# Decoder step on one core: the samples' softmax tail in more pieces, the first mixer chunk and a memory weight split among the sample batches, the last sum of squares behind the first query

## The chip, the core and the metric

The kernel runs on one core of a Trainium2 chip. The core has five engines that work side by side and wait for each other by semaphores: TensorE (PE, matrix products and transposes, with its weight loads listed as PEld), VectorE (DVE), ScalarE (ACT), GpSimd (POOL) and SyncE (SP), which here issues nearly all DMAs. Matrix products write into PSUM, a small memory of eight banks that PE, DVE and ACT can reach. Everything else works in SBUF, 128 partitions wide. Each engine takes its instructions in a fixed order, so an instruction that waits holds up all that is behind it on that engine.

The metric is the time of one execution on the device, in microseconds (us). The median of three runs before the change is 1881.3 us (1880.76 to 1881.76).

## The reference

One layer of a hybrid decoder, for a prompt of 1024 tokens and for eight samples of four new tokens each, 1056 tokens together, with a model width of 1024. All is float32. What matters here:

```python
def rms_norm(x, g):
    xf = x.astype(jnp.float32)
    y = xf * lax.rsqrt(jnp.mean(xf * xf, axis=-1, keepdims=True) + EPS)
    return (y * g.astype(jnp.float32)).astype(x.dtype)

def masked_attend(q, k, v, q_pos, k_pos):
    s = jnp.einsum('...qhd,...khd->...hqk', q, k).astype(jnp.float32) * (QK_HEAD ** -0.5)
    s = jnp.where(k_pos[None, :] <= q_pos[:, None], s, NEG_INF)
    p = jax.nn.softmax(s, axis=-1).astype(v.dtype)
    return jnp.einsum('...hqk,...khd->...qhd', p, v)

def mla_sample_attend(q, ckv_n, kpe, pool_ckv, pool_kpe, page_table, w_uk, w_uv, g_qk_k):
    ...
    def one(args):
        pages, q1, c1, pe1 = args
        c_all = jnp.concatenate([pool_ckv[pages].reshape(PAST_LEN, KV_LORA), c1.astype(pool_ckv.dtype)], axis=0)
        pe_all = jnp.concatenate([pool_kpe[pages].reshape(PAST_LEN, QK_ROPE), pe1.astype(pool_kpe.dtype)], axis=0)
        k, v = mla_keys_values(c_all, pe_all, k_pos, w_uk, w_uv, g_qk_k)
        return masked_attend(q1, k, v, q_pos, k_pos)

def merge_out(a_out, b_out, g_out_a, g_out_b, w_o):
    return jnp.concatenate([rms_norm(a_out, g_out_a), rms_norm(b_out, g_out_b)], axis=-1) @ w_o

def mem_kv(mem, g_mem_in, w_mk, w_mv, g_mk):
    n, m, _ = mem.shape
    hm = rms_norm(mem, g_mem_in)
    k = rms_norm((hm @ w_mk).reshape(n, m, MEM_HEADS, MEM_HEAD_DIM), g_mk)
    v = (hm @ w_mv).reshape(n, m, MEM_HEADS, MEM_HEAD_DIM)
    return k, v

def mem_attend(h, mk, mv, w_mq, g_mq, w_mo):
    n, t, _ = h.shape
    q = rms_norm((h @ w_mq).reshape(n, t, MEM_HEADS, MEM_HEAD_DIM), g_mq)
    ...
```

For each sample the keys of 4096 past positions are rebuilt from paged latents (32 pages of 128 positions), normalised per head and compared with the four new queries of eight heads. The layer then merges the gMLP group (a) and the attention group (b) through `w_o`, attends to 256 memory tokens (`mem_kv`, `mem_attend`), and ends in a gated feed-forward with a short convolution.

## The kernel before

**Precision.** A product in full float32 is made of three products of split operands: each operand is a rounded high half and a low half (the remainder), and `mm3` (L185) adds high x high, high x low and low x high. The high half is a copy on ACT (L191, or L195 with a gain), the low half a subtraction on DVE (L192, L198). So each operand must be split before PE can use it.

**Stages in order of time.** The input projections and the gMLP group (`phase1`), the prompt's attention (`phase2a`), the samples' attention in eight batches of 16 steps (`phase2b`), the memory's keys and values (`mem_kv`), the mixed output projection (`mixed`, `out_proj`), the memory attention (`mem_attention`), the feed-forward (`ffn`).

**The sample loop.** A batch is one sample. A page holds 128 positions and is called a group; a step treats two groups, four pages make a quad (two steps). In `phase2b` the order on PE, ACT, DVE and POOL is written out by hand: `at(n, pos, f)` puts a piece of work at step n and at a position within it (from -2 to 3; the scores stand between 1 and 2, the products with the values between 2 and 3). The order on SP is left to a planner. Per step: PE makes the scores from the quad's split latents (tiles ch for the high, cl for the low half, against w2h and w2l) into the PSUM tiles s; ACT squares them (L1272, L1275), DVE adds the rope part (L1274) and reduces the squares (L1278). Per quad: four page loads each of cT (transposed latents, three buffers) and ck (latents as values, a ring of fifteen buffers), the cast to ch on ACT (L1231), the subtraction to cl half on POOL and half on DVE (L1235), and the key rotation krq on POOL (L1220 to L1222). PE reads POOL's half of cl in the third matmul of a quad's first step.

**The softmax of a batch** is `batch_softmax`, in pieces r = 0 to 10 at steps counted from the batch's first. The norms of the first 24 groups come at steps 12 to 14, their scaling on POOL at 14 (L1296), their peak at 15. The last eight groups' norm starts at 16; at position 2 of step 16 it is finished, with scaling, peak and maximum (mx, L1323). PE transposes the peaks at the start of step 18 (L1326), DVE reduces them at its end, and at the end of step 19 PE spreads the maximum to all partitions (L1334), ACT copies it (L1336) and POOL subtracts it from the scores (L1337, 128 x 1056). ACT takes the exponential at step 20. Since a batch has 16 steps, steps 16 to 20 lie in the next batch. The products with the values follow four steps after the batch, from step 23 on (L1346, L1348). The last batch's pieces behind step 16 run after the loop.

**Between the stages.** The mixers' outputs go through a DRAM tensor (`mix_dram`, written by `mix_steps` in pairs of token tiles, L1505). After the loop, `mem_kv` begins: the memory weights' tiles and the memory itself are loaded into four places of the ck ring in the last steps (L1113). `mixed` then loads `mix_dram` back in three chunks of 384, 384 and 288 tokens (L1530, three `raw` buffers shared with the weights) and splits them into mx0, mx1 and mx2. `out_proj` runs over the eight output tiles, for each the three chunks, adds the squares of the result per chunk in `acc` (ACT L1591, POOL L1592), and at its end makes the sums over the width for all three chunks on PE (L270) and their inverse roots `r3` on DVE (`rsqrt`, L222 to L236), in the PSUM banks o, m and o again. `mem_attention` starts with `query(0, 0)`, whose PSUM tile b takes over the bank o.

## Time and profile before

| | us |
|---|---|
| median of three runs | 1881.3 |
| profiled execution, its own time | 1887.48 |
| its span, first to last instruction | 1885.8 |
| TensorE busy | 1822.9 |
| the sample loop, about 427 to 892 | 465 |
| memory keys and values, to the first chunk of the mixer, about 892 to 934 | 42 |
| mixed output projection, to the first query, about 934 to 1042 | 108 |

The profile is of one execution, and its rows use its own clock from the first instruction. In a row of the timeline stand the start, the duration, the engine, the line, the operation, the tile written and the tiles read; in square brackets stand the engine's idle time before it and what ended it. "A <- B" in a list of waits says that A waited for B. TensorE's granted clock was 0.985 of full speed on average over the span. Where the prediction needs lines, they are shown there.

### The profile page before, as it was taken

To read this page: it belongs to the slowest core of one execution; us is meant where nothing else is said; L and a number is where in the kernel's file an instruction comes from. 1 tells how busy PE (TensorE), PEld (TensorE's weight loads), DVE (VectorE), ACT (ScalarE), POOL (GpSimd) and SP (SyncE) were. 2 spreads that over 40 slices of the span, in tenths; PEclk is the share of its full clock that TensorE was granted. 3 is DMA by queue.
4 is the path that set the end of the run, shared out by engine and by line. 5 is a ranking of instruction groups with operands and counts; after the bars stand their busy time and mean duration, and the time that the engine had idled before them with its cause. 6 is when DMAs were issued, how large, how long until landed. Compare 5 with 4: busy or idle time off the path is not lost.

```text
span 1885.8 us, 39848 instructions
## 1 busy us (share of the span) xinstructions
PE 1822.9 (97%) x14402; PEld 1757.2 (93%) x14402; DVE 1380.2 (73%) x2883; ACT 927.5 (49%) x1965; POOL 715.1 (38%) x826
## 2 busy tenths in 40 slices
PE   6999899989999999999999999999999999999999
PEld 6999799889999999998799988999999999999999
DVE  6865967766777667776654676788888888879664
ACT  6435676666555555555443355633332333344442
POOL 1221515643544455444213100157677677500000
PEclk9999899999999999999999999999999999999999
DMA  8102204666765665664564335322222222395252
GB/s 294 60 10 69 80 1 163 228 223 186 213 196 167 187 179 169 175 170 148 171 177 134 134 134 163 128 80 69 91 69 94 77 69 80 99 363 164 79 153 76
DMA packets 135559, 260.18 MB, mean 138 GB/s; under 512 B 20417, under 2 KB 78626, under 8 KB 132290
## 3 DMA queue, kind: packets, MB, share of 16 engines
q1 hardware_dynamic: 134498, 256.58, 43.4%
q8 instruction: 114, 1.87, 0.4%
q10 hardware_dynamic: 864, 1.05, 0.2%
q14 instruction: 83, 0.68, 0.1%
HBM read 212.27 MB, written 45.30 MB: 137 GB/s over the span
## 4 chain that ended last, share of the span: by engine, by line
PE 60%; DVE 6%; issue 4%; DMA 3%; POOL 2%; SPq 1%; ACT 1%; POOLq 0%; DVEq 0%; ACTq 0%
PE d L185 12%; PE s L185 11%; PE b L185 7%; PE F L185 7%; PE X L185 6%; PE E L185 6%; PE A L185 3%; PE y L185 3%; DMA cT<-cT 1%; PE o L1348 1%; DVE mx L1299 1%; POOL S L1296 1%; PE t L185 1%; PE v L185 1%; SPq L1207 1%
## 5 line engine op out<-in xcount | busy, mean ns | idle before, releaser
L185 PE MATMUL s<-w2h,ch 128*128 128x288 f32 (+1 forms) x1024 | 303.8, 297 | 0.0
L185 PE MATMUL s<-w2h,cl 128*128 128x288 f32 (+1 forms) x1024 | 295.1, 288 | 2.7 <-POOL cl L1235 1.4
L185 PE MATMUL s<-w2l,ch 128*128 128x288 f32 (+1 forms) x1024 | 294.7, 288 | 0.0
L185 PEld LDWEIGHTS s<-w2h,ch 128*128 128x128 f32 x1024 | 192.6, 188 | 10.8 <-issue 8.3
L185 PEld LDWEIGHTS s<-w2h,cl 128*128 128x128 f32 x1024 | 192.4, 188 | 3.4 <-POOL cl L1235 1.9
L185 PEld LDWEIGHTS s<-w2l,ch 128*128 128x128 f32 x1024 | 192.8, 188 | 0.0
L1278 DVE TENSOR_REDUCE ss<-sq 128x16 f32<-128x1024 f32 x128 | 155.6, 1215 | 49.3 <-ACT sq L1275 48.4
L1235 POOL TENSOR_TENSOR cl<-cT,ch 128x512 fp32r<-128x512 f32 x64 | 83.7, 1307 | 160.7 <-ACT ch L1231 128.9
L1275 ACT ACTIVATE sq<-s 128x512 f32<-128x512 f32 x128 | 76.5, 598 | 90.0 <-PE s L185 90.0
L1272 ACT ACTIVATE sq<-s 128x512 f32<-128x512 f32 x128 | 76.8, 600 | 78.0 <-PE s L185 78.0
L191 ACT CAST a<-brb 128x528 fp32r<-128x528 f32 x77 | 48.8, 634 | 111.0 <-PE d L185 107.1
L185 PE MATMUL mm<-whi,xh 128*128 128x256 f32 (+3 forms) x288 | 84.5, 294 | 14.4 <-ACT xh L195 9.8
L185 PE MATMUL d<-a,w 128*128 128x264 f32 x768 | 95.4, 284 | 1.0 <-DVE G L2064 1.0
L192 DVE TENSOR_TENSOR a<-brb,a 128x528 fp32r<-128x528 f32 x77 | 54.4, 707 | 57.2 <-ACT a L191 57.1
L185 PEld LDWEIGHTS d<-a,w 128*128 128x128 f32 x768 | 94.3, 188 | 1.1 <-issue 1.1
L185 PE MATMUL mm<-wlo,xh 128*128 128x256 f32 (+3 forms) x288 | 83.3, 292 | 0.0
L185 PE MATMUL mm<-whi,xl 128*128 128x256 f32 (+3 forms) x288 | 83.2, 293 | 0.0
L930 PEld LDWEIGHTS o<-v,pth 128*128 128x128 f32 x576 | 75.9, 197 | 7.3 <-ACT pth L920 5.2
L930 PE MATMUL o<-v,pth 128*128 128x64 f32 x576 | 76.2, 274 | 4.8 <-ACT pth L920 4.4
L1935 POOL TENSOR_TENSOR lo<-s,hi 128x1024 fp32r<-128x1024 f32 x20 | 63.0, 3148 | 45.7 <-ACT hi L1934 45.7
L1231 ACT CAST ch<-cT 128x512 fp32r<-128x512 f32 x128 | 73.5, 627 | 3.9 <-DMA cT<-cT 3.9
L1990 ACT COPY a<-A 128x264 f32<-128x264 f32 x43 | 16.1, 375 | 118.7 <-PE A L185 114.9
(714 smaller groups left out, 6472.2 us busy)
## 6 DMA issues: line engine op xcount, KB each, us to landing
cT<-cT SPq DMA_DIRECT2D x256, 160.0 KB, 2.5
ck<-ck SPq DMA_DIRECT2D x256, 144.0 KB, 3.4
raw<-w_up SPq DMA_DIRECT2D x44, 512.0 KB, 3.6
wsumd<-wsum SPq DMA_DIRECT2D x13, 1024.0 KB, 4.3
actd<-cv SPq DMA_DIRECT2D x44, 264.0 KB, 2.6
brb<-actd SPq DMA_DIRECT2D x44, 264.0 KB, 5.9
wsum<-w_down SPq DMA_DIRECT2D x11, 1024.0 KB, 5.2
raw<-wsumd SPq DMA_DIRECT2D x20, 512.0 KB, 3.8
```

Source lines behind the costliest of these rows:

```text
L185: self.nc.tensor.matmul(out, l, r, start=first and i == 0, stop=last and i == len(seq) - 1)
L191: {"act": nc.scalar.copy, "pool": nc.gpsimd.tensor_copy, "dve": nc.vector.tensor_copy}[eng](hi, src)
L192: low = lambda: nc.vector.tensor_tensor(lo, src, hi, ALU.subtract)
L930: nc.tensor.matmul(u["o"][:, e], th[:, z * P : z * P + P], s["v"][:, jj, h % 4], start=j == z == 0, stop=e == 1 and jj == 2 * G + 1)
L1207: nc.sync.dma_start(ck[j * 32 : j * 32 + 32], I["ck"][bass.ds(rv, 1)].rearrange("a t s f -> (a t) s f"))
L1231: nc.scalar.copy(d["h"][:, k], src[k])
L1235: (nc.vector if k else nc.gpsimd).tensor_tensor(d["l"][:, k], src[k], d["h"][:, k], ALU.subtract)
L1272: nc.scalar.activation(sq[:, 0], ps[:, :, n0 : n0 + 256], AF.Square)
L1275: nc.scalar.activation(sq[:, 1], pt.rearrange("p (e d) -> p e d", e=2), AF.Square)
L1278: yield lambda: nc.vector.tensor_reduce(s["ss"][:, g0 : g0 + 2].rearrange("p e (z h) -> p z e h", z=2), sq.rearrange("p z e (h d) -> p z e ...
L1296: e.tensor_tensor(x, x, ss[:, g0:g1].rearrange("p g h -> p (g h)").unsqueeze(2).broadcast_to([P, n, 4]), ALU.mult)
L1935: eng.tensor_tensor(lo, src, hi, ALU.subtract)
```

## The change

1. `batch_softmax` has thirteen pieces instead of eleven. The last eight groups' norm starts at step 16, has its second part at the start of 17, its third at the end of 17, and scaling, peak and maximum come at the end of step 18. The transpose moves to step 19, the reduction of the peaks to 20, the spreading with POOL's subtraction to the end of step 20, the exponential to step 21. The closing of a batch's output moves by one step.
2. The first mixer chunk (mx0) is loaded and split in the sample loop: four loads into the ck ring at steps 20, 36, 52 and 68, eight splits at relative steps 8 and 10 of the batches that follow. `mixed` leaves it out. The first memory weight is loaded first of the four last loads and split two steps before the loop's end. `mix_steps` writes each token tile to DRAM by itself.
3. The sums and roots of the third chunk leave `out_proj` and stand behind `query(0, 0)`, in another PSUM bank; its `acc` lies in another pool. In `mem_kv` the ring of diagonal tiles has three buffers instead of four, and two small tiles of the samples' memory attention share a buffer with another.

```diff
@@ phase2b
-        hl = self.t(p, [P, 4, 288], F32, "ck", 15).rearrange("p k n -> p (k n)")[:, :1024].rearrange("p (k n) -> p k n", k=4)
+        hl = self.t(p, [P, 4, 288], F32, "ck", 15).rearrange("p k n -> p (k n)")[:, :1024].rearrange("p (m k n) -> p m k n", m=2, k=4)
+        hl = [hl[:, i] for i in range(2)]
...
+        self.mx0 = [self.t(px, [P, 8, 384], FR, f"mx0{x}") for x in "hl"]
+        wk0 = [self.t(px, [P, 8, P], FR, f"wk0{x}") for x in "hl"]
...
+        place = lambda: self.t(p, [P, 4, 288], F32, "ck", 15).rearrange("p k n -> p (k n)")
+
+        def mixed_load(k):
+
+            raw = place()[:, :768].rearrange("p (k n) -> p k n", k=2)
+            nc.sync.dma_start(raw, self.mix_dram[:, k : k + 2, :384])
+            for e in range(2):
+                at(8 * k + 24 + 2 * e, 3, lambda e: self.split(*(x[:, k + e] for x in self.mx0), raw[:, e], self.col("g_ab", k + e)), e)
+
+        for k in range(0, 8, 2):
+            at(8 * k + 20, 0, mixed_load, k)
+        at(last - 2, 3, lambda: self.split(*wk0, raws[0].rearrange("p (k n) -> p k n", k=8)))
...
-            for r, (k, pos) in enumerate(((12, 0), (13, 0), (14, 0), (14, 3), (15, 0), (16, 0), (16, 2), (18, 0), (18, 3), (19, 2), (20, 2))):
+            for r, (k, pos) in enumerate(((12, 0), (13, 0), (14, 0), (14, 3), (15, 0), (16, 0), (17, 0), (17, 3), (18, 2), (19, 2), (20, 0), (20, 2), (21, 3))):
...
-            for k, pos, f in ((0, 3, tail[0]), (1, 2, tail[1]), (3, 3, tail[2])):
+            for k, pos, f in ((0, 3, tail[0]), (2, 2, tail[1]), (4, 3, tail[2])):
...
-                    src = (I["memT"][:, :4], I["memT"][:, 4:], I["w_mk"][0], I["w_mk"][1])[len(raws)]
+                    src = (I["w_mk"][0], I["memT"][:, :4], I["memT"][:, 4:], I["w_mk"][1])[len(raws)]
@@ batch_softmax
         elif r == 5:
             s["it"] = norms(24, 32, nc.gpsimd if final else nc.vector)
             next(s["it"])
+        elif r == 6:
             next(s["it"])
-        elif r == 6:
+        elif r == 7:
             for _ in s["it"]:
                 pass
+        elif r == 8:
             scale(nc.vector, 24, 32)
             peak(1, 24, 33)
...
@@ mem_kv
-            w = self.stream(I["w_mk"][h], 8, raw=raws[2 + h].rearrange("p (k n) -> p k n", k=8) if h < 2 else None)
+            w = wk0 if h == 0 else self.stream(I["w_mk"][h], 8, raw=raws[3].rearrange("p (k n) -> p k n", k=8) if h == 1 else None)
...
-                dg = self.t(p, [P, P], F32, "diag", 4)
+                dg = self.t(p, [P, P], F32, "diag", 3)
@@ mix_steps
-            nc.vector.tensor_copy(hl[:, :, i * tn : i * tn + tn], tp)
+            nc.vector.tensor_copy(hl[i][:, :, :tn], tp)
+            o = t0 + i * tn
+            nc.sync.dma_start(self.mix_dram[:, z * 4 : z * 4 + 4, o : o + tn], hl[i][:, :, :tn])
             if nt is None and i < m - 1:
                 yield
-        nc.sync.dma_start(self.mix_dram[:, z * 4 : z * 4 + 4, t0 : t0 + w], hl[:, :, :w])
@@ mixed
-                for k in range(0, 8, 2):
+                for k in range(0, 8 if c else 0, 2):
@@ out_proj
-        for c in range(3):
-            st = self.t(self.ppt, [P, 512], F32, "om"[c % 2], 1)
-            self.tok_sums(st, acc[c], c, self.ones)
-            ct = slice(3 * c, 3 * c + 3)
-            self.rsqrt(p, r3[:, ct], st[:, ct], 1.0 / 1024)
+        for c in range(2):
+            self.token_roots(p, self.t(self.ppt, [P, 512], F32, "om"[c], 1), r3, c)
+
+    def token_roots(self, p, st, r3, c):
+        self.tok_sums(st, self.acc[c], c, self.ones)
+        ct = slice(3 * c, 3 * c + 3)
+        self.rsqrt(p, r3[:, ct], st[:, ct], 1.0 / 1024)
@@ mem_attention
+        roots = self.t(pp, [P, 512], F32, "sx", 1)
...
                 if h == 0 and c == 0:
+                    self.token_roots(p, roots, r3, 2)
                     memory()
```

More of the change, by code (lines that the diff above doesn't have):

```diff
@@ L487, in mix @@
         def mix(i0):
-            hl = self.t(pl, [P, 4, 256], F32, "hl")
+            hl = self.t(pl, [P, 2, 4, P], F32, "hl")
+            hl = [hl[:, i] for i in range(2)]
             self.mix_group(pl, pp, 0, i0, min(i0 + 2, 9), lambda i: a_all[:, i], hl, lambda j: self.t(pl, [P, 512], F32, "csq", 4), ("st", 3))
@@ L701, in mix @@
                 hl = hls.pop()
+                hl = [hl[:, :, a : a + P] for a in (0, P)]
                 nt = lambda j: self.t(p, [P, 2, 4, 96], F32, "k", 4).rearrange("p m h d -> p (m h d)")[:, :512]
@@ L1050, in phase2b @@
         pa = self.pa3 = self.open("p3a", side="right")
-        pt, p = self.open("p3t"), self.open("p3")
+        pt, px, p = self.open("p3t"), self.open("mx"), self.open("p3")
+        self.mx0 = [self.t(px, [P, 8, 384], FR, f"mx0{x}") for x in "hl"]
+        wk0 = [self.t(px, [P, 8, P], FR, f"wk0{x}") for x in "hl"]
         ppt, pp = self.open("ps3t", space=PSUM), self.open("ps3", space=PSUM)
@@ L1071, in run @@
                 f()
-        hl = self.t(p, [P, 4, 288], F32, "ck", 15).rearrange("p k n -> p (k n)")[:, :1024].rearrange("p (k n) -> p k n", k=4)
+        hl = self.t(p, [P, 4, 288], F32, "ck", 15).rearrange("p k n -> p (k n)")[:, :1024].rearrange("p (m k n) -> p m k n", m=2, k=4)
+        hl = [hl[:, i] for i in range(2)]
         mix = self.mix_steps(pa, ppt, 1, 6, 8, lambda i: self.b_last[:, i % 2], hl, None, ("m", 1))
@@ L1110, in steps @@
                 if n > last - 8 and n % 2 == 0 and len(raws) < 4:
-                    raw = self.t(p, [P, 4, 288], F32, "ck", 15).rearrange("p k n -> p (k n)")[:, : 8 * P]
-                    src = (I["memT"][:, :4], I["memT"][:, 4:], I["w_mk"][0], I["w_mk"][1])[len(raws)]
+                    raw = place()[:, : 8 * P]
+                    src = (I["w_mk"][0], I["memT"][:, :4], I["memT"][:, 4:], I["w_mk"][1])[len(raws)]
                     nc.sync.dma_start(raw.rearrange("p (k n) -> p k n", n=src.shape[2]), src)
@@ L1145, in phase2b @@
             self.wp = self.open("w", bufs=3, side="right")
-            mem = self.mem_kv(raws)
+            mem = self.mem_kv(raws, wk0)
             for f in late:
@@ L1323, in batch_softmax @@
             nc.vector.tensor_tensor(s["m"][:, 0], s["m"][:, 0], s["m"][:, 1], ALU.max)
-        elif r == 7:
+        elif r == 9:
             tp = s["tp"] = self.t(pp, [P, 512], F32, "m", 1)
             nc.tensor.transpose(tp[:32, :P], s["m"][:, 0], self.ident)
-        elif r == 8:
+        elif r == 10:
             mm = self.t(p, [32, 1], F32, "mm", 2)
@@ L1331, in batch_softmax @@
             nc.vector.tensor_scalar(s["dg"], self.ident[:32, :32], mm, None, ALU.mult)
-        elif r == 9:
+        elif r == 11:
             bc = self.t(pp, [P, 512], F32, "m", 1)[:, :32]
@@ L1385, in stream, with mem_kv @@
         return hi, lo
-    def mem_kv(self, raws):
+    def mem_kv(self, raws, wk0):
         nc, tc, I, O = self.nc, self.tc, self.I, self.O
@@ L1397, in mem_kv @@
         acc = self.t(p, [P, 256], F32, "acc")
-        mr = [r.rearrange("p (k n) -> p k n", k=4) for r in raws[:2]]
+        mr = [r.rearrange("p (k n) -> p k n", k=4) for r in raws[1:3]]
         xs = [(mh[:, k], ml[:, k]) for k in range(8)]
@@ L1488, in mix_steps @@
             ns.append(n)
-            o = n if nt else hl[:, 2 * (i - i0) : 2 * (i - i0) + 2].rearrange("p k n -> p (k n)")[:tn]
+            o = n if nt else hl[i - i0][:tn].rearrange("p k n -> p (k n)")
             nc.scalar.activation(o, src(i)[:tn], AF.Square, accum_out=r[:, i - i0 : i - i0 + 1])
@@ L1492, in mix_steps @@
         self.rsqrt(p, r, r, 1.0 / 512)
-        w = m * tn
         yield
@@ L1501, in mix_steps @@
                 nc.tensor.transpose(tp[:, k], n[:, k * P : k * P + P], self.ident[:tn, :tn])
-            nc.vector.tensor_copy(hl[:, :, i * tn : i * tn + tn], tp)
+            nc.vector.tensor_copy(hl[i][:, :, :tn], tp)
+            o = t0 + i * tn
+            nc.sync.dma_start(self.mix_dram[:, z * 4 : z * 4 + 4, o : o + tn], hl[i][:, :, :tn])
             if nt is None and i < m - 1:
                 yield
-        nc.sync.dma_start(self.mix_dram[:, z * 4 : z * 4 + 4, t0 : t0 + w], hl[:, :, :w])
     def mixed(self):
         nc, I = self.nc, self.I
-        px = self.open("mx")
         pm = self.pm = self.open("pm")
-        mxs = [None] * 3
-        for c in (0, 2, 1):
+        mxs = [self.mx0, None, None]
+        for c in (2, 1):
             o, n = CH[c]
             if c == 1:
-                self.acc = [self.t(pm, [P, 384], F32, f"acc{e}") for e in range(3)]
+                self.acc = [self.t(pm, [P, 384], F32, f"acc{e}") for e in range(2)]
                 self.t(pm, [P, 384], F32, "sqx", 3)
-            mxs[c] = [self.t(px if c == 0 else pm, [P, 8, n], FR, f"mx{c}{x}") for x in "hl"]
+            mxs[c] = [self.t(pm, [P, 8, n], FR, f"mx{c}{x}") for x in "hl"]
         ws = {}
@@ L1708, in sample_values @@
                 nc.tensor.transpose(tp[:, k], sample["p"][:, 0, k * P : k * P + P], self.ident)
-            pT = self.t(ps_, [P, 2, P], F32, "pT")
+            pT = self.t(ps_, [P, 1, 256], F32, "pf").rearrange("p a (k n) -> p (a k) n", k=2)
             nc.vector.tensor_copy(pT, tp)
@@ L1725, in sample_values @@
                         )
-            sd = self.t(ps_, [P, P], F32, "sd")
+            sd = self.t(ps_, [P, 1, 256], F32, "pf")[:, 0, :P]
             nc.scalar.copy(sd, so)
@@ L2238, in build @@
     r3 = N.t(xp, [P, 9], F32, "r3")
+    N.acc.append(N.t(xp, [P, 384], F32, "acc2"))
     po = N.open("po")
```

## The prediction

> **What bounds the kernel now.** The first view is the page: span and the engines' busy row.

> ```profile
> span 1885.8 us, 39848 instructions
> PE 1822.9 (97%) x14402; PEld 1757.2 (93%) x14402; DVE 1380.2 (73%) x2883; ACT 927.5 (49%) x1965; POOL 715.1 (38%) x826
> ```

> TensorE (PE) is busy for 1822.9 of 1885.8 us. The change adds and removes no matmul, so it can act in only two ways: on the 62.9 us in which PE stands idle, and on the stretches in which PE is busy at a lower granted clock. The second view is therefore the list of PE's waits (who waited for whom: total, times, longest).

> ```profile
> PE m L1326 <- DVE mx L1323: 6.3, 7, 0.9
> PE b L185 <- DVE r L236: 2.7, 1, 2.7
> PE b L185 <- DVE ml L198: 1.7, 3, 1.2
> PE o L1545 <- ACT n L1542: 1.4, 1, 1.4
> PE b L185 <- ACT mx0h L195: 1.1, 1, 1.1
> PE o L270 <- POOL acc L1592: 1.1, 1, 1.1
> PE b L185 <- ACT mx1h L195: 0.9, 1, 0.9
> PE b L185 <- DVE mx0l L198: 0.2, 1, 0.2
> ```

> The three edits each name a row: the transpose of the peaks (mx) in seven of the eight sample batches, the first mixer chunk (mx0) after them, and the sums of squares (acc, then r) before the first query. The third view, the table by stretches, gives PE's busy time and the clock around two of them (columns: stretch, length, PE, PEld, DVE, ACT, POOL busy, clock, DMA share, GB/s).

> ```profile
> 490.00:892.00 402.00, 394.22 (x3319) 371.03 (x3317) 294.54 (x562) 223.73 (x493) 193.59 (x306) 1.00 0.62 175
> 934.00:936.70 2.70, 1.41 (x9) 1.07 (x8) 1.41 (x3) 1.12 (x2) 0.00 (x0) 1.00 0.99 346
> 936.70:943.50 6.80, 5.87 (x20) 5.30 (x20) 3.65 (x6) 4.13 (x7) 0.00 (x0) 0.50 0.67 187
> 1039.10:1045.90 6.80, 4.20 (x13) 4.23 (x14) 6.49 (x26) 2.94 (x3) 1.39 (x1) 0.50 0.89 274
> ```

> In the batches the clock is full. After each of the other two groups of gaps (the second ends in the rows of part 3) PE is granted half its clock for 6.8 us, so a gap there costs more than its own length.

> **Part 1, the samples' softmax.** The last eight groups' norm, scaling and peak were two pieces on VectorE (DVE), two half-steps apart, and PE's transpose asked for the peaks at the start of relative step 18. Now there are four pieces at steps 16, 17 (twice) and 18, and the transpose asks at the end of step 19. The timeline of batch 3 shows the old order on DVE and PE.

> ```profile
> 663.31 1.11 DVE L1289 TENSOR_TENSOR ss<-ss,kss 128x64 f32<-128x64 f32 x1
> 669.08 0.19 DVE L1323 TENSOR_TENSOR mx<-mx 128x32 f32<-128x32 f32 x1
> 669.33 0.28 PE L1326 MATMUL m<-ident,mx 128*32 128x128 f32 x1 [0.92 <-DVE mx L1323]
> ```

> The work takes 5.96 us from 663.31 to 669.27. In the new order the steps' own DVE work comes between. All that DVE did from the start of this work to the last matmul of step 19 is in one row of the table by stretches:

> ```profile
> 663.30:675.60 12.30, 11.38 (x93) 11.17 (x91) 11.06 (x26) 5.88 (x13) 5.57 (x10) 1.00 0.64 182
> ```

> DVE was busy for 11.06 us. PE will ask at 674.7 (675.60 less the 0.92 saved), 11.4 us after 663.3. So the peaks are there 0.3 us early even if all of that work went before them, and some of it (step 19's own reduction) goes behind. The seven waits, 6.3 us, go.

> What is late next is on GpSimd (POOL). The broadcast, and the subtraction behind it, move from the end of step 19 to the end of step 20. Step 19 was followed by two whole steps before PE needed POOL's next result, the low half (cl) of the next quad. Step 20 is followed by one. This is the same batch.

> ```profile
> 675.41 1.93 SPq L1203 DMA_DIRECT2D cT<-cT  x4
> ...
> 675.60 0.28 PE L185 MATMUL s<-w2h,cl 128*128 128x256 f32 x1
> 675.81 0.40 PE L1334 MATMUL m<-dg,ones 32*128 32x32 f32 x2
> 676.14 1.07 PE L1348 MATMUL o<-ck,S 128*32 128x257 f32 x16
> 676.67 2.47 POOL L1337 TENSOR_TENSOR S<-S,bc 128x1056 f32<-128x1056 f32 x1 [1.11 <-ACT bc L1336]
> ...
> 679.11 1.28 POOL L1235 TENSOR_TENSOR cl<-cT,ch 128x512 fp32r<-128x512 f32 x1
> ...
> 680.16 0.28 PE L185 MATMUL s<-w2h,cl 128*128 128x256 f32 x1
> 680.42 0.47 PE L1250 MATMUL s<-bd,krq 128*128 128x128 f32 x2
> 680.64 0.38 PE L185 MATMUL s<-w2h,ch 128*128 128x288 f32 x1
> ...
> 683.75 0.30 PE L185 MATMUL s<-w2h,ch 128*128 128x288 f32 x1
> 684.02 0.29 PE L185 MATMUL s<-w2h,cl 128*128 128x288 f32 x1
> ```

> Take as zero the start of the step's last matmul. POOL's cl is finished 4.79 us later (679.11 + 1.28 - 675.60); with the 0.06 us that PE took to resume in batch 0 (cl done at 491.76, PE at 491.82, below) that is 4.85. PE, from the last matmul of step 20, does the broadcast (676.14 - 675.60 = 0.54), the rope matmul (680.64 - 680.42 = 0.22), a step (683.75 - 680.64 = 3.11), the fold matmul, which stands between these two now and moves behind the step (680.42 - 680.16 less the usual spacing of 0.12 = 0.14), and two matmuls (0.27) before the first that reads cl: 4.28. So PE waits about 0.57 us in each batch, 4.0 us in seven. That POOL can be late for this operand is seen once in the trace of before, where its scaling ran late:

> ```profile
> 490.50 1.26 POOL L1235 TENSOR_TENSOR cl<-cT,ch 128x512 fp32r<-128x512 f32 x1
> 491.82 0.40 PE L185 MATMUL s<-w2h,cl 128*128 128x288 f32 x1 [1.44 <-POOL cl L1235]
> ```

> Bounds per batch: 0, if POOL gets to it earlier, and 1.2, with the 0.6 by which an operand of this shape was at most late. I take 0.57. Part 1 is 6.3 - 4.0 = **2.3 us gained**.

> **Part 2, the first chunk and the weight moved into the batches.** Four loads, eight pairs of splits, and one wide pair move. Their rows, and that of the page loads beside them (KB of one, median us to landing):

> ```profile
> cT<-cT SPq DMA_DIRECT2D x256, 160.0 KB, 2.5
> raw<-mix SPq DMA_DIRECT2D x8, 384.0 KB, 3.8
> L195 ACT ACTIVATE mx0h<-raw,cols x8: 599/600/615, 926.0 to 935.0; 128x384 fp32r<-128x384 f32 x8
> L198 DVE SCALAR_TENSOR_TENSOR mx0l<-raw,cols,mx0h 128x384 fp32r<-128x384 f32 x8 | 4.7, 615 | 1.7 <-ACT mx0h L195 1.7
> ```

> In the batches that is 0.60 us of ScalarE (ACT) and 0.61 of DVE in relative steps 8 and 10, before the softmax starts at 12. Of 402 us DVE is busy 294.5 and ACT 223.7, so a step of some 3.5 us has about 0.9 us of DVE free and 1.5 of ACT. I cost it at nothing. Without that cover it would be at most 8 x 0.6 = 4.9 us. The loads take places in the ring of fifteen page buffers, so SyncE (SP) must wait for releases up to three steps later than now; this is a rival below. On SP each load is one issue; writing the mixer chunks by token tile makes 17 issues of 9, spread over 280 us: nothing.

> The wide split leaves the head of the memory stage, where PE waits 1.2 us for ml; but the second weight's load starts only once a page buffer is free, and is not moved. The bounds are 0 and 1.2; I take 0.

> In the mixer stage three waits go: 1.08 + 0.21 + 0.93 = 2.2 us (1.1, 0.2 and 0.9 in the list). What should replace them is the second chunk (mx1), whose loads stood behind the four that are gone and now come that much earlier. With the gaps I count the half-clock stretch behind them: 5.87 us busy at 0.50 is 2.9 us lost. Part 2 is **5.1 us gained**, between 0 (the wait only moves) and 6.5 (the later wait for n, 1.4 us, goes too).

> [...]

> **Part 3, the last sums of squares.** The end of the output projection:

> ```profile
> 1035.72 0.72 PE L270 MATMUL o<-ones,acc 128*128 128x1 f32 x6
> 1036.31 0.81 PE L270 MATMUL m<-ones,acc 128*128 128x1 f32 x6
> 1038.17 0.83 PE L270 MATMUL o<-ones,acc 128*128 128x1 f32 x6 [1.06 <-POOL acc L1592]
> 1041.70 0.66 PE L185 MATMUL b<-xh,hi 128*128 128x384 f32 x1 [2.70 <-DVE r L236]
> ```

> The third group waits for POOL's last addition, and the query then waits for DVE to read that group's bank (o). With the third group behind the first query both waits go: 1.06 + 2.70 = 3.8 us. The query's weight was ready long before:

> ```profile
> 999.03 1.23 DVE L192 TENSOR_TENSOR lo<-raw,hi 128x1024 fp32r<-128x1024 f32 x1 [0.50 <-ACT hi L191]
> ```

> This is its low half, 40 us earlier. The query's first bank is no longer one that DVE reads. Nothing is late next: POOL's addition ends before 1038.2, and the query covers it. Half clock from 1039.1 to 1045.9 goes with the idle: 4.20 us busy at 0.50 is 2.1 us. Part 3 is **5.9 us gained**, 0 at the least if the bank still waits.

> **The sum.** 2.3 + 5.1 + 5.9 = 13.3 us from the profiled execution's 1887.5 us (span 1885.8, 1.7 around it). The runs' median is 1881.3, 6.2 us (0.3%) below that; I subtract the same microseconds: **1868.0 us**.

> **Rivals.**
> - POOL is not late in part 1 (bound 0): 13.3 + 4.0 = 17.3, 1864.0 us. For it: in seven of eight batches POOL met its deadline after the scaling. Against it: the 0.57 above. Chance 0.17.
> - The mixer wait only moves to mx1 or to the output weights, clock and all: 2.3 + 5.9 = 8.2, 1873.1 us. For it: mx1 is waited for already, 0.9 us. Against it: its loads come earlier. Chance 0.15.
> - The softmax edit does not do what it says: DVE misses its margin (0.3 us at the least), the waits stay and POOL's come on top: 11.0 - 4.0 = 7.0, 1874.3 us. Chance 0.07.
> - Half clock does not go with these gaps: 13.3 - 2.9 - 2.1 = 8.3, 1873.0 us. For it: the wait of 1.44 us at 490 was followed by full clock. Against it: both stretches follow idle time at once. Chance 0.07. [...]
> - Slower: the page ring. Each of four loads takes a place for six steps, so nine later loads (three mixer, six page) wait for a buffer up to three steps longer, and the next quad's cT queues behind them on SP. I reckon that cT lands some 6.4 us after such a release (two groups of four issues at the 1.93 above, landing 2.5), two steps before its use. Of these 6.4 us POOL's split needs 1.3 and ACT's cast before it, an estimate, as much: 4 us to spare. If landings come 5.9 us later still, PE loses 1.9 us nine times, 17.1: 1885.1 us. Against it: loads are issued several steps ahead, and SP's order is not fixed by hand. Chance 0.08.

> **How the numbers follow.** The forecast has 0.46; its own range is 1864 to 1871. The range 1860 to 1877 reaches from all gains at once (6.3 + 6.5 + 5.9 + 1.2 = 19.9, 1861.4 us) to the moved waits; it leaves out the slower case and the tails. A measurement of this kernel tells 0.2%, 3.8 us, from no change. Faster than 1877.5 are the forecast and all rivals but the last, less some tail: 0.85. The same 0.07, slower 0.08.

> **What would show it.** The list of waits after: no row of m on mx; instead s on POOL's cl about seven times, some 0.6 us each, at relative step 22. No row of b on mx0h, and clock 1.00 at the first output chunks. The first query directly behind the second group of sums, with clock 1.00. Waits of ACT for the mixer loads, or of PE on krq, in the batches would make me wrong towards slower; batches with no wait at all, towards faster.

## The result, and the profile after

| | before | after |
|---|---|---|
| median | 1881.73 us (6 runs, 1880.76 to 1884.43) | 1870.86 us (6 runs, 1867.60 to 1873.69) |
| profiled execution, own time | 1887.48 us | 1873.17 us |

The ratio is 0.9939, with a 95% interval of 0.9928 to 0.9951. The medians differ by 10.9 us; by the ratio it is 11.5 us. The forecast was 1868.0 us, 13.3 us faster. The page of the kernel after, span and busy row:

```profile
span 1871.5 us, 39806 instructions
PE 1812.4 (97%) x14402; PEld 1746.4 (93%) x14402; DVE 1382.2 (74%) x2883; ACT 928.9 (50%) x1965; POOL 708.0 (38%) x826
```

PE is busy for 10.5 us less with the same number of matmuls. Of this, 5.0 us lie in the four stretches cut below, in which PE had half clock for 17.1 us before and for none after. The rest, 5.6 us, lies ahead of these stretches, where half clock took 37.6 us in the trace of before and 30.7 in that of after; the kernel before alone varies as much there (30.7 us in two more traces), so this is no gain of the change. PE's list of waits after, those that bear on the change:

```profile
PE s L185 <- POOL cl L1252: 3.0, 8, 0.7
PE m L1179 <- ACT olT L1389: 2.2, 1, 2.2
PE b L185 <- DVE ml L198: 1.6, 2, 1.4
PE o L1563 <- ACT n L1560: 1.3, 1, 1.3
PE b L1479 <- DVE diag L1478: 1.1, 3, 0.7
PE s L1267 <- POOL krq L1239: 1.1, 2, 0.6
PE b L185 <- ACT mh L195: 0.9, 1, 0.9
```

No row of m on mx is left, none of b on mx0h, none of o on acc or b on r. New are seven more waits for cl, and those for olT and diag (before, the matmuls on diag waited 0.7 us for kr). To see what each part was worth, the span is cut at five matmuls that every version has. This is the table by stretches of the kernel before, then of the kernel after: the batches from the first score matmul of batch 1 to the last one; the memory stage, to the first matmul on mx0h; the mixer's output projection, to the first sum; the sums with the queries, to a matmul late in the second query.

```profile
489.96:890.08 400.12, 392.34 (x3286) 370.06 (x3285) 292.66 (x559) 222.13 (x490) 193.63 (x306) 1.00 0.62 175
890.08:930.52 40.44, 36.87 (x293) 29.41 (x291) 28.70 (x70) 24.12 (x47) 15.31 (x22) 1.00 0.52 163
930.52:1035.72 105.20, 101.29 (x619) 98.88 (x618) 52.42 (x96) 40.93 (x82) 24.86 (x22) 0.95 0.55 165
1035.72:1051.52 15.80, 12.04 (x65) 11.90 (x64) 11.24 (x41) 4.68 (x7) 2.69 (x2) 0.78 0.90 309
```

```profile
488.76:885.87 397.11, 394.15 (x3287) 370.46 (x3285) 294.64 (x565) 228.97 (x499) 186.05 (x305) 1.00 0.64 180
885.87:928.25 42.38, 37.57 (x292) 29.69 (x291) 31.78 (x74) 24.03 (x47) 14.77 (x22) 1.00 0.56 178
928.25:1027.84 99.59, 96.00 (x618) 95.00 (x618) 46.31 (x85) 35.86 (x73) 25.01 (x22) 1.00 0.49 149
1027.84:1037.65 9.81, 9.81 (x65) 9.81 (x64) 9.57 (x32) 4.57 (x7) 2.72 (x2) 1.00 0.81 276
```

The first number behind each stretch is its length: 3.0, 5.6 and 6.0 us gained in the batches, the mixer stage and the sums, and 1.9 us lost in the memory stage, where the forecast had nothing. In the three traces of the kernel before, the batches and the memory stage, in which no half clock falls, repeat to 0.3 us. The experiments' traces are cut in the same way:

| kernel (one trace each) | batches | memory | mixer | sums, queries |
|---|---|---|---|---|
| before | 400.12 | 40.44 | 105.20 | 15.80 |
| before, again | 400.11 | 40.39 | 102.05 | 16.50 |
| before, again | 399.87 | 40.43 | 102.58 | 16.16 |
| softmax only | 397.29 | 40.45 | 104.92 | 15.94 |
| mixer only | 399.77 | 42.04 | 98.77 | 15.93 |
| sums only | 400.36 | 40.39 | 102.00 | 9.81 |
| filled gaps | 400.51 | 40.51 | 103.22 | 14.30 |
| after | 397.11 | 42.38 | 99.59 | 9.81 |
| after without weight | 398.00 | 41.69 | 98.97 | 9.81 |
| after, two ring places | 397.86 | 42.03 | 99.53 | 9.81 |
| after, split loads | 398.26 | 44.17 | 98.94 | 9.81 |
| after, subtraction later | 394.05 | 42.26 | 99.38 | 9.81 |
| after, values later | 397.85 | 42.08 | 96.73 | 9.81 |
| after, both moves | 392.93 | 42.32 | 96.43 | 9.81 |

### The profile page after: what moved, and what is told of

It is laid out like the page before. It is cut to its first block, busy times and chain, and to the rows that moved or that the text cites. A ratio compares the mean times of both kernels' runs of the same rounds, so it can differ in the third digit from the quotient of the medians.

```text
span 1871.5 us, 39806 instructions
## 1 busy us (share of the span) xinstructions
PE 1812.4 (97%) x14402; PEld 1746.4 (93%) x14402; DVE 1382.2 (74%) x2883; ACT 928.9 (50%) x1965; POOL 708.0 (38%) x826
## 4 chain that ended last, share of the span: by engine, by line
PE 61%; issue 5%; SPq 3%; DMA 3%; DVE 3%; POOL 2%; ACT 1%; POOLq 0%; DVEq 0%; ACTq 0%
PE d L185 12%; PE s L185 11%; PE b L185 7%; PE F L185 7%; PE X L185 6%; PE E L185 6%; PE A L185 3%; PE y L185 3%; DMA cT<-cT 2%; SPq L1220 2%; SPq L1224 1%; PE o L1367 1%; PE t L185 1%; POOL cl L1252 1%; PE v L185 1%
## 5 line engine op out<-in xcount | busy, mean ns | idle before, releaser
L185 PE MATMUL s<-w2h,ch 128*128 128x288 f32 (+1 forms) x1024 | 303.7, 297 | 0.0
L185 PE MATMUL s<-w2h,cl 128*128 128x288 f32 (+1 forms) x1024 | 296.0, 289 | 4.2 <-POOL cl L1252 3.0
L185 PE MATMUL s<-w2l,ch 128*128 128x288 f32 (+1 forms) x1024 | 294.6, 288 | 0.0
L185 PEld LDWEIGHTS s<-w2h,ch 128*128 128x128 f32 x1024 | 192.6, 188 | 8.3 <-ACT sq L1292 2.5
L185 PEld LDWEIGHTS s<-w2h,cl 128*128 128x128 f32 x1024 | 192.4, 188 | 6.5 <-POOL cl L1252 5.0
L185 PEld LDWEIGHTS s<-w2l,ch 128*128 128x128 f32 x1024 | 192.8, 188 | 0.0
L1289 ACT ACTIVATE sq<-s 128x512 f32<-128x512 f32 x128 | 76.7, 600 | 74.5 <-PE s L185 74.0
L191 ACT CAST a<-brb 128x528 fp32r<-128x528 f32 x77 | 48.8, 634 | 111.4 <-PE d L185 107.9
L185 PE MATMUL mm<-whi,xh 128*128 128x256 f32 (+3 forms) x288 | 83.4, 291 | 16.4 <-ACT xh L195 10.0
L192 DVE TENSOR_TENSOR a<-brb,a 128x528 fp32r<-128x528 f32 x77 | 54.3, 707 | 58.3 <-ACT a L191 58.3
L185 PE MATMUL d<-a,w 128*128 128x264 f32 x768 | 95.4, 284 | 0.5 <-DVE G L2087 0.5
L185 PEld LDWEIGHTS d<-a,w 128*128 128x128 f32 x768 | 94.3, 188 | 0.7 <-issue 0.7
L185 PE MATMUL mm<-wlo,xh 128*128 128x256 f32 (+3 forms) x288 | 82.1, 288 | 0.0
L185 PE MATMUL mm<-whi,xl 128*128 128x256 f32 (+3 forms) x288 | 82.1, 289 | 0.0
L1958 POOL TENSOR_TENSOR lo<-s,hi 128x1024 fp32r<-128x1024 f32 x20 | 62.9, 3142 | 45.7 <-ACT hi L1957 45.7
L2013 ACT COPY a<-A 128x264 f32<-128x264 f32 x43 | 16.1, 375 | 118.7 <-PE A L185 113.9
```

Source lines behind the costliest of these rows:

```text
L185: self.nc.tensor.matmul(out, l, r, start=first and i == 0, stop=last and i == len(seq) - 1)
L191: {"act": nc.scalar.copy, "pool": nc.gpsimd.tensor_copy, "dve": nc.vector.tensor_copy}[eng](hi, src)
L192: low = lambda: nc.vector.tensor_tensor(lo, src, hi, ALU.subtract)
L1289: nc.scalar.activation(sq[:, 0], ps[:, :, n0 : n0 + 256], AF.Square)
L1958: eng.tensor_tensor(lo, src, hi, ALU.subtract)
```

## The experiments

**One part at a time.** Three versions make one part of the change alone on the kernel before: the softmax pieces with the tail's positions; the mixer chunk with the weight, the writes by tile and the diag ring of three; the sums with the bank for the roots. Their diffs are the parts of the change shown above. The fourth is the kernel after with the weight put back:

```diff
-        wk0 = [self.t(px, [P, 8, P], FR, f"wk0{x}") for x in "hl"]
-        at(last - 2, 3, lambda: self.split(*wk0, raws[0].rearrange("p (k n) -> p k n", k=8)))
...
-                    src = (I["w_mk"][0], I["memT"][:, :4], I["memT"][:, 4:], I["w_mk"][1])[len(raws)]
+                    src = (I["memT"][:, :4], I["memT"][:, 4:], I["w_mk"][0], I["w_mk"][1])[len(raws)]
...
-            w = wk0 if h == 0 else self.stream(I["w_mk"][h], 8, raw=raws[3].rearrange("p (k n) -> p k n", k=8) if h == 1 else None)
+            w = self.stream(I["w_mk"][h], 8, raw=raws[2 + h].rearrange("p (k n) -> p k n", k=8) if h < 2 else None)
```

> The kernel before with the softmax pieces and the tail positions of the change alone. Theory: the seven waits for mx (6.3 us) go, and PE waits for POOL's cl at relative step 22 in seven batches, 0.57 us each by the forecast or about 0.33 each as in the trace of after: 2.3 to 4.0 us faster than before. Rival that POOL is never late: 6.3 us faster, no wait of s on cl but the one of batch 0. Rival that DVE misses its margin: rows of m on mx stay, 0 us or slower. The half-clock stretches in the mixer stage (near 937) and behind the output projection (near 1039) should both still be there, a few us earlier than before.

> The kernel before with the first mixer chunk and the first memory weight moved into the batches alone. Theory: no wait of b on mx0h or mx0l (2.2 us), full clock behind the first output chunk (2.9 us), but a wait of m on olT of about 2.2 us in the second chunk as in the trace of after: between 2.9 and 5.1 us faster. The half-clock stretch near 1039 stays, seven waits for mx stay. If the short half-clock stretch near 960.6 also hangs on this part, up to 1.7 us more. Rival that the wait only moves, clock and all: 0 us. Rival of the page ring: waits of s on krq in the batches and no gain or slower.

> The kernel before with the last sum of squares behind the first query alone. Theory: the waits of o on acc (1.1 us) and of b on r (2.7 us) go and half clock from 1039.1 to 1045.9 goes with them (2.1 us): 5.9 us faster. Rival that the clock stretch has another cause and stays: 3.8 us faster, the query at half clock. Rival that the bank still waits: 0 us. The waits for mx and mx0h and the half clock near 937 stay.

> The kernel after, but the first memory weight is loaded third and split in the head of the memory stage as before. Theory: moving it is worth nothing, so about 11.4 us faster than before, as the whole change, and PE's waits in the head of the memory stage add up to about 2.4 us instead of 3.0. Rival that the wide split's place is worth its bound of 1.2 us: 10.2 us faster. Rival that the move costs 0.6 us: 12.0 us faster. The total may not tell these apart; the waits of b on mh and ml in the trace should.

Measured against the kernel before (median 1883.78 us, 26 runs): softmax only 1880.35 us, ratio 0.9980 (0.9968 to 0.9993), by the ratio 3.8 us faster; mixer only 1879.26 us, 0.9981 (0.9968 to 0.9993), 3.6 us faster; sums only 1876.55 us, 0.9971 (0.9957 to 0.9984), 5.5 us faster; after without the weight 1869.98 us, 0.9934 (0.9918 to 0.9950), 12.4 us faster. By the medians alone it would be 3.4, 4.5, 7.2 and 13.8 us. By the ratios the three parts add up to 12.9 us, against 11.5 for the whole, which agrees within the intervals. The lengths in the table are sharper: softmax 397.29 against 400.1 in the batches, sums 9.81 against about 16.1, and the mixer part shortens its own stage while it lengthens the memory stage by 1.6 us. Without the weight that stage is still 1.3 us longer than before, but 0.7 shorter than in the trace of after; the waits for mh, ml and the second weight in its head add up to 2.6 us, against 2.4 to 2.8 in the three traces of before and 3.0 after. The lengths say it more clearly: from the last score matmul to the first matmul on diag, the main part of the stage, all seven traces without the weight's move take 37.1 to 37.2 us, and all seven with it 37.7. So the weight's move cost some 0.6 us rather than gaining up to 1.2; the medians can't tell that apart.

The mixer part alone missed one thing that was expected of it: half clock fell at its first output chunks too, for 3.4 us from 927.2 on, and its wait for olT was 0.7 us, not 2.2.

The sums' trace also held a surprise. Its mixer stage is that of before, with the same waits, and not one stretch of half clock fell into it (granted clock 1.00 over its 102.00 us). So half clock did not belong to those gaps alone.

**The kernel before, twice more,** unchanged.

> The kernel before, unchanged, profiled once more. In the traces so far every change of the granted clock lies on a grid of 3.413 us whose phase against the program's start differs from run to run (1.44 us in the trace of before, 1.94 in that of the sums alone), and half clock follows a grid window in which PE idles for more than about 1.8 us. Theory: the gaps of the mixer stage and of the third sum (about 2.2 and 3.8 us) are the same in every run of this kernel, but whether half clock follows depends on how the grid cuts them: the stretches near 937, 960 and 1039 us need not all come again. Rival: the gaps alone bring it, and all three stretches are there again with 6.8, 3.4 and 6.8 us.

> As the run ahead of it: the kernel before, unchanged, with a third phase of the grid. Theory: another set of stretches, each behind a window with more than about 1.8 us idle (between 1.0 and 1.8 us it may go either way). Rival: the same three stretches as in the first trace of before.

One run each: 1884.29 and 1880.75 us. The stretches came at 938.2 to 941.6 and 1037.2 to 1044.0 in the one, at 934.0 to 937.4 and 1032.9 to 1039.8 in the other: near the mixer's first chunk half as long as in the first trace, near 960 none, behind the sums again 6.8 us. In the table by stretches, the windows of the 3.413 us grid, first two of the first trace (half clock in the second), then two of the sums-only trace (no half clock behind either):

```profile
933.28:936.70 3.42, 2.13 (x12) 1.37 (x10) 1.61 (x5) 1.12 (x2) 0.00 (x0) 1.00 0.99 350
936.70:940.11 3.41, 2.48 (x9) 1.91 (x9) 1.90 (x3) 2.32 (x4) 0.00 (x0) 0.50 0.50 147
```

```profile
930.36:933.78 3.42, 2.21 (x11) 1.40 (x9) 1.67 (x5) 1.12 (x2) 0.00 (x0) 1.00 0.91 292
933.78:937.19 3.41, 2.20 (x12) 1.74 (x12) 2.13 (x5) 2.15 (x3) 0.00 (x0) 1.00 0.78 246
```

PE's busy time in the window ahead of half clock, 2.13 us, is nearly that of the two in the sums-only trace, 2.21 and 2.20, behind which full clock goes on. So the theory holds in that the same kernel has other stretches in each trace; the rival (the gaps alone) holds for the sums only. What decides between windows as alike as these is not shown; the last section counts how often each side came.

**The gaps filled.** The kernel before with ten matmuls added in the two waits at the end of the output projection; nobody reads their result.

```diff
+        def fill(n):
+            ps = self.t(pp, [P, 512], F32, "b", 6)[:, :384]
+            for i in range(n):
+                self.nc.tensor.matmul(ps, xh[:, i, :P], xh[:, i, :384], start=i == 0, stop=i == n - 1)
...
-            self.tok_sums(st, acc[c], c, self.ones)
+            with self.tc.manual_schedule(engines={mybir.EngineType.PE}):
+                if c == 2:
+                    fill(3)
+                self.tok_sums(st, acc[c], c, self.ones)
+                if c == 2:
+                    fill(7)
```

> The kernel before with ten matmuls of 128x384 added whose result nobody reads: three ahead of the third group of sums (about 1.0 us of its wait of 1.06) and seven behind it (about 2.4 us of the query's wait of 2.70). All waits stay where they were, PE is only kept busy in them. Theory: PE now idles less than 1 us in any window of the clock's grid there, so the half clock from 1039.1 to 1045.9, which came in all three traces of before, does not come, and the first query takes about 2.1 us less: 2.1 us faster than before, although work was added. Rival that the half clock has another cause: it comes again near 1039, 0 us or slightly slower.

1879.76 us against 1882.54 us, ratio 0.9986 (0.9975 to 0.9997): by the ratio 2.6 us faster with more work, and in the trace the stretch of sums and queries is 14.30 instead of about 16.1 us long. Half clock did not go altogether: one window of it was left, where two had been. The table by stretches of this kernel shows the window ahead of it, the window at half clock and the next; then the timeline's rows from the first of them:

```profile
1030.43:1033.84 3.41, 2.98 (x21) 2.66 (x22) 3.24 (x15) 0.78 (x2) 1.83 (x2) 1.00 0.60 210
1033.84:1037.26 3.42, 2.89 (x10) 2.41 (x9) 3.25 (x21) 2.52 (x3) 0.86 (x1) 0.50 0.84 237
1037.26:1040.67 3.41, 3.41 (x22) 3.41 (x21) 3.30 (x5) 0.42 (x1) 0.00 (x0) 1.00 1.01 414
```

```profile
1030.39 0.81 PE L270 MATMUL m<-ones,acc 128*128 128x1 f32 x6
1031.06 0.78 PE L1570 MATMUL b<-xh 128*128 128x384 f32 x3
1032.26 0.83 PE L270 MATMUL o<-ones,acc 128*128 128x1 f32 x6 [0.43 <-POOL acc L1602]
```

PE is idle for only 0.43 us in that window, and half clock still follows. But a good part of its busy time is the sums, matmuls of 128x1: for 1.75 us of the window PE ran no matmul of 64 or more columns. The last section counts the windows of all traces by this time. In this trace, filling the gaps took away a part of the half clock: 3.4 us are left of the 6.8 in each of the three traces of before.

**Where POOL's waits come from.** POOL's subtraction goes behind the next quad's cl, half a step later.

```diff
-            ... (20, 0), (20, 2), (21, 3))):
+            ... (20, 0), (20, 2), (21, 0), (21, 3))):
...
             nc.scalar.copy(s["bc"], bc)
+        elif r == 12:
             (nc.vector if final else nc.gpsimd).tensor_tensor(S, S, s["bc"].unsqueeze(1).broadcast_to([P, 33, 32]), ALU.subtract)
```

> The kernel after, but POOL's subtraction of the peaks is issued at the start of step 21, behind that step's cl, instead of at the end of step 20; the broadcast and the exponential stay. Theory: the seven waits of s on POOL's cl at relative step 22 (2.3 us in the trace of after) go, and nothing takes their place: 13.8 us faster than the kernel before instead of 11.5. Rival that the wait goes to the next user of POOL (a wait of s on krq, whose three operations now stand behind the subtraction) or to the exponential (o on S): 11.5 us or less.

1866.41 us against 1881.76 us, ratio 0.9910 (0.9893 to 0.9927): 15.4 us faster than before at the medians (16.9 by the ratio), where 13.8 were expected. POOL's rows in batch 3, of the kernel after and then of this one:

```profile
676.91 2.46 POOL L1356 TENSOR_TENSOR S<-S,bc 128x1056 f32<-128x1056 f32 x1 [6.99 <-DMA cT<-cT]
679.32 1.29 POOL L1252 TENSOR_TENSOR cl<-cT,ch 128x512 fp32r<-128x512 f32 x1
```

```profile
669.63 1.30 POOL L1252 TENSOR_TENSOR cl<-cT,ch 128x512 fp32r<-128x512 f32 x1 [4.21 <-ACT ch L1248]
672.43 2.47 POOL L1357 TENSOR_TENSOR S<-S,bc 128x1056 f32<-128x1056 f32 x1 [1.50 <-ACT bc L1355]
```

With cl ahead of the subtraction the seven waits are gone, and hardly anything took their place (one wait of 0.4 us for dg in the first of these batches): the batches take 394.05 us here and 392.93 with both moves below, on average 4.2 us less than the 397.73 that is the mean of the six versions with the new softmax and the subtraction first. But the matmuls' list shows these seven waits as 2.3 us only (seven of 0.27 to 0.53). The weight loads' list of the kernel after, and PE's and PEld's timeline at one of the waits, say why:

```profile
PEld s L185 <- POOL cl L1252: 5.0, 9, 0.9
```

```profile
680.10 0.29 PE L185 MATMUL s<-w2l,ch 128*128 128x288 f32 x1
680.67 0.40 PE L185 MATMUL s<-w2h,cl 128*128 128x288 f32 x1 [0.28 <-POOL cl L1252]
680.91 0.30 PE L185 MATMUL s<-w2h,ch 128*128 128x288 f32 x1
```

```profile
680.67 0.19 PEld L185 LDWEIGHTS s<-w2h,cl 128*128 128x128 f32 x1 [0.51 <-POOL cl L1252]
```

cl is the operand that PE loads as weights, so it is the weight load that waits, 0.51 us. The matmul ahead started at 680.10, and its record of 0.29 us covers the first part of the wait; with the usual distance of 0.13 us between starts, the distance of 0.57 lost 0.44, and the first matmul behind the stall takes 0.24 to the next start instead of 0.13. Together 0.55 us, twice what the matmuls' list shows, and what the forecast had (0.57).

**The page ring.** Two ways of taking more of its places for the early mixer loads.

```diff
+            place()
             raw = place()[:, :768].rearrange("p (k n) -> p k n", k=2)
```

```diff
-            raw = place()[:, :768].rearrange("p (k n) -> p k n", k=2)
-            nc.sync.dma_start(raw, self.mix_dram[:, k : k + 2, :384])
+            raw = [place()[:, :384] for e in range(2)]
             for e in range(2):
+                nc.sync.dma_start(raw[e], self.mix_dram[:, k + e, :384])
```

> The kernel after, but each of the four early mixer loads takes two places of the ring of fifteen page buffers instead of one (the second is left empty, no transfer is added). Theory: the ring had room for one more place and little beyond; with two, three quads (23, 31 and 39) get their buffer seven steps (about 24 us) after the time of issue, when their split is already due, and the mixer splits hold ACT's queue as well: waits of s on krq or cl and of ACT on raw or cT near 545, 605 and 660 us, 20 to 80 us slower than the kernel after. Rival that the ring is not a limit at all: no change, 11.5 us faster than before. A small loss (under 10 us) would say that loads issued late catch up faster than reckoned.

> The kernel after, but each of the four early mixer loads is two loads of half the size, and each half takes a ring place of its own that its split uses. In the run with an empty second place, ACT began to split each quad just as long after SP had issued its load as in the kernel after (9.2 us at the least), so the empty place took no buffer's turn. Theory: a place that is used does; the least time from a quad's load issue to its first split falls from about 9 us towards the 2.8 us of a landing or below the work behind it, and where it does PE waits: 0 to 20 us slower than the kernel after (11.5 us faster than before to 8 slower), with waits of ACT for cT or raw<-mix in the batches. Rival that the ring is not a limit: the least time stays about 9 us and nothing changes.

1870.07 us, ratio 0.9929 (0.9914 to 0.9944), and 1870.31 us, 0.9932 (0.9910 to 0.9955): as the kernel after. The first expectation of 20 to 80 us slower was far off. From quad 18 on, the least time from SP's issue of a quad's last cT load to ACT's first cast of it was 12.8 us before, 9.4 after, 9.1 with the empty places and 9.3 with the split loads. So the change did take 3.4 us of this lead, and 9.4 are over three times the 2.8 us of a landing (the page of after). Why further places take no more of it is open; the count of places behind the first expectation does not hold. In its single trace the version with split loads has the longest memory stage, 44.17 us, with 6.8 us of half clock from 929.4 on; its runs as a whole are not slower.

**The new wait for olT.** The matmuls that read it (`end[1]`, cut off from `end`) go behind the third chunk; then both moves at once.

```diff
-        end()
+        end[0]()
...
                 chunk(m, 0)
+                if m == 1:
+                    end[1]()
                 chunk(m, 1)
```

> The kernel after, but the sixteen matmuls of the samples' values (wuv), which wait for olT inside the second output chunk, are issued behind the third chunk. Theory: the wait of m on olT (2.2 us in the trace of after) goes, as ACT then has about 6 us more for the mx2h splits and the olT copy: 13.7 us faster than before. Rival that it only moves: the chain from these matmuls to the transposes of n is now shorter in time, so the wait of o on n (1.3 us) grows by as much, 11.5 us faster.

> The kernel after with both moves (the subtraction behind cl, the wuv matmuls behind the third chunk). Theory: the two are far apart and add up: 16.0 us faster than before. Rival: 11.5 us or less.

1867.84 us, ratio 0.9922 (0.9905 to 0.9938), 13.9 us faster at the medians (13.7 expected), and with both moves 1864.97 us, ratio 0.9905 (0.9889 to 0.9922), 16.8 us faster than the kernel before at the medians (16.0 expected). The mixer stage shrinks from 99.2 (mean of the six versions that have the new mixer stage and this order) to 96.73 and 96.43 us, and neither the wait for olT nor the one for n is left in it. The version with both moves beats both kernels.

## Why the prediction was right or wrong

| term | forecast | measured |
|---|---|---|
| part 1, batches | 2.3 gained (6.3 - 4.0) | 2.4 gained |
| part 2, memory stage | 0 (0 to 1.2 gained) | 2.0 lost |
| part 2, mixer stage | 5.1 gained (2.2 waits, 2.9 clock) | 4.1 gained |
| part 3 | 5.9 gained (3.8 waits, 2.1 clock) | 6.3 gained |
| sum | 13.3 | 10.8 (medians: 10.9) |

Measured are differences of means of the table of stage lengths: batches 400.12 (six versions with the old softmax) to 397.73 (six with the new one and the subtraction first); memory 40.44 (six without the mixer part) to 42.47 (seven with it and the weight); mixer 103.33 to 99.20 (six each, without the two in which the values stand later and the one without the weight counted to the new); sums 16.07 (five, without the filled gaps) to 9.81.

**Part 1 was right in both terms.** DVE kept its margin, the seven mx waits went, and POOL became late at the place foretold, by 0.55 us in the wait taken apart above, where 0.57 was reckoned; undoing that lateness alone gave 4.2 us against 4.0. The reading that might have misled stands above: by the matmuls' list of waits one would have thought it half as large.

**Part 2 was mis-sized, and this is the step that failed: 0 for the memory stage, with 0 to 1.2 us gained as its bounds, and "I cost it at nothing" for what moves.** The stage lost 2.0 us (1.75 without the trace of the split loads), in two places. The first is its main part, up to diag, which the weight's move makes 0.6 us longer, as shown above: PE now waits 0.9 us for mh, where it waited 0.2. The second is its end. From the first matmul on diag to the first on mx0h PE took 3.3 us in all six traces with the old mixer stage; it takes 4.7 in the trace of after, 4.3 to 4.6 in six others, and 6.4 with the split loads. The second chunk's loads come earlier, as the forecast said, and so do its splits, which now stand here. But splits of the first chunk stood here before. DVE's rows, first before, then after, with others between them left out:

```profile
924.49 0.87 DVE L1459 TENSOR_SCALAR diag<-ident,r 128x128 f32<-128x128 f32 x4
928.37 0.48 DVE L1459 TENSOR_SCALAR diag<-ident,r 128x128 f32<-128x128 f32 x2
928.77 0.61 DVE L198 SCALAR_TENSOR_TENSOR mx0l<-raw,cols,mx0h 128x384 fp32r<-128x384 f32 x1
929.69 0.28 DVE L1459 TENSOR_SCALAR diag<-ident,r 128x128 f32<-128x128 f32 x1
```

```profile
921.86 0.68 DVE L1478 TENSOR_SCALAR diag<-ident,r 128x128 f32<-128x128 f32 x3
925.20 0.62 DVE L198 SCALAR_TENSOR_TENSOR mx1l<-raw,cols,mx1h 128x384 fp32r<-128x384 f32 x1
925.74 0.47 DVE L1480 SCALAR_TENSOR_TENSOR kr<-kr,cols,b 128x256 f32<-128x256 f32 x1
926.13 0.28 DVE L1478 TENSOR_SCALAR diag<-ident,r 128x128 f32<-128x128 f32 x1
926.33 0.61 DVE L198 SCALAR_TENSOR_TENSOR mx1l<-raw,cols,mx1h 128x384 fp32r<-128x384 f32 x1
926.86 0.28 DVE L1478 TENSOR_SCALAR diag<-ident,r 128x128 f32<-128x128 f32 x1
```

PE needs eight diags in turn. Before, four were ready ahead and only the last came behind a split; after, the ring of three lets three be ready, and each of the last two comes behind a split. On ACT the copy of oo, for which PE did not wait before, comes behind splits as well (0.3 us in the trace of after). The forecast has no term for the shorter ring. Whether the ring of three or the splits' new time costs the 1.0 to 1.4 us was not tried, and stays open.

The mixer stage itself did better on waits than reckoned, although a wait came in for olT (2.2 us in the trace of after, 0 to 1.7 in the other five with this order): the rival of the moved wait in another place. The sums-only trace, without half clock, has 102.00 us there, 2.8 more than the mean after, where 2.2 were reckoned; with the 1.3 us of clock below that is the 4.1 of the table. The weight loads show it better than the matmuls: their waits in the stage add up to 6.9 us in the sums-only trace and to 4.4 in that of after. ACT's rows show the new wait's origin:

```profile
937.79 0.91 ACT L195 ACTIVATE mx2h<-raw,cols 128x256 fp32r<-128x256 f32 x2 [1.44 <-DMA raw<-mix]
938.61 0.19 ACT L1389 COPY olT<-m 128x64 f32<-128x64 f32 x1
```

The copy of olT stands behind the third chunk's splits, which wait for their load. The forecast looked only at who waits for mx1, not at what is queued behind the splits on ACT.

**The clock term of part 2 was a single draw.** 2.9 us came from one trace with 6.8 us of half clock near the first chunk; the six traces with the old mixer stage had 0 to 10.2 us of it in the whole stage (mean 4.5), and their mean of 103.33 us lies 1.3 above the trace without any. The new versions are not free of half clock either. It fell at the first output chunks in two of the eight (3.4 us in mixer only, 6.8 with the split loads). In five of the seven with the weight's move one window of it fell into the memory stage, near its start (granted clock 0.94 to 0.96 over these stages, 1.00 over the other two). That the trace of after has none is luck in part. It cost nothing that the lengths show: four of these five memory stages (42.0 to 42.3 us, the split loads apart) are no longer than the two without half clock (42.3 and 42.4). Part 3's stretch, 6.8 us, came in every trace with the old sums and its gaps unfilled, and 2.1 was about the right size for it: 6.3 gained less 3.8 of waits leaves 2.5; the first query runs at full clock behind the second group of sums, as the timeline of the kernel after has it:

```profile
1028.42 0.81 PE L270 MATMUL m<-ones,acc 128*128 128x1 f32 x6
1029.10 0.42 PE L185 MATMUL b<-xh,hi 128*128 128x384 f32 x1
```

**The rivals.** That half clock stays did not happen in the trace of after. The ring had its lead shortened and no wait from it. The signs foretold all came: mx gone, cl at relative step 22 seven times (0.3 to 0.5 us each in the list, where 0.6 was said), full clock at the first output chunks, no krq wait past the first batch. The new waits in the memory stage and for olT were not on that list.

## What to carry to other kernels

When a load is moved out of a stage, follow the loads behind it too: they come earlier, and the work that they release can land between instructions that someone waits for. A ring of buffers that is made shorter needs a term in the sum too, if only to rule it out. Read what a stall costs from the distance between the starts of instructions, or from the weight load's wait, not from the idle time before the matmul alone: at the wait taken apart above these show 0.55, 0.51 and 0.28 us. A half-clock stretch seen in one trace is a draw: of the gaps that this change touches, only those of the old sums brought it each time that they were left unfilled, 6.8 us in five of five traces.

## What the runs showed of the hardware that was not expected

| such time in a window | windows | followed by half clock |
|---|---|---|
| under 1.2 us | 7284 | 0 |
| 1.2 to 2.0 us | 117 | 26 |
| 2.0 us or more | 57 | 57 |

In the traces of before and after alone it is 1041 windows and 0, 16 and 3, 8 and 8. What decides between 1.2 and 2.0 us was not shown.

**Half clock behind windows with little idle time.** By idle time alone, 7,275 windows have under 1.0 us, and half clock followed two of them: that of the filled gaps (0.43 us) and one of 0.98 us. In the window of the filled gaps another 1.32 us lie in the sums' matmuls of 128x1. Whether their width is the reason was not shown; no run varied it by itself.
